# Finishing rows of an expert mixture: one VectorE step in place of two GpSimd steps, GpSimd's work in program order, four buffers for the running sums

## The chip, the core and the metric

The kernel runs on one core of one Trainium2 chip. Its time is the device time of one execution in microseconds. The core has five engines with queues of their own: TensorE (PE, with its weight loads PEld), VectorE (DVE), ScalarE (ACT), GpSimd (POOL) and SyncE (SP). Each runs its queue in order, and waits at the head of it for semaphores of the others. DMAs are issued from the queues (here SP's and POOL's) and run beside the engines.

## The reference, cut to what matters

One decoder layer over 4096 tokens of width 1024: retention and gated DeltaNet heads, an output projection, and then a mixture of experts. The change touches only the mixture and the final norm:

```python
gate = p_group * p_exp / jnp.sum(p_exp, axis=-1, keepdims=True)      # 2 of 32 experts for each token
hid = jax.nn.silu(lax.ragged_dot(xs, w1, group_sizes)) * lax.ragged_dot(xs, w3, group_sizes)
ys = lax.ragged_dot(hid.astype(xs.dtype), w2, group_sizes) * gate.reshape(-1)[order][:, None]
ffn = jax.ops.segment_sum(ys, tok, num_segments=n)                   # the two experts' rows of a token are added
x = x + gate2[:, None, :] * ffn
return rmsnorm(x, final_norm_w)                                      # x * rsqrt(mean(x*x) + 1e-6) * final_norm_w
```

So a token is finished when its second expert has been added: then its row is scaled by one over its root mean square and multiplied by a weight vector.

## The kernel before

Every product is made in three passes over values split into a high and a low part (`split`, L69 to L72: ACT rounds to the high part, DVE subtracts). The expert stage, `phase_d`, is the last of four, and runs from about 2640 us to the end.

The 32 experts are ranked by how many tokens chose them, and each rank has a fixed capacity of rows, from 832 down to 128. They run in the order largest, smallest, second largest, second smallest, and so on. An expert's rows are cut into tiles of up to 128 rows and these into chunks of up to 384 rows, that is 1 to 3 tiles. In the first part of the stage chunks of 256 rows are mixed with experts of one tile of 128 rows; in the last third chunks of 3 tiles (288 or 320 rows) alternate with chunks of 2 tiles (240 rows).

For each chunk:

- `d_gather`: POOL issues one indirect DMA per tile that gathers the chunk's input rows (`xg`, three buffers), L1340. It is called one chunk ahead.
- `d_turn`: PE transposes the rows (`ptx`, L1356), ACT and DVE split them into `xh` and `xl`.
- `d_hidden`: PE multiplies with w1 and w3 (`ph`, L1385 to L1387, or L1414 to L1416 for a tile of 128 rows); ACT and DVE make the hidden values `hs`, `hh`, `hl`. At two points in it, `job` takes up to two waiting pieces of work each.
- `d_acc`: POOL gathers, per tile, the running sums of the chunk's tokens (`ag`, 128 x 1040, L1433) from `acc_d`. Column 1024 says whether the token has been seen. `ag` has three buffers ("rooms").
- `d_to`: POOL works out from that column two row numbers (`to`, L1446 to L1449): one for `acc_d`, one for the output; one of them is always out of range, and the DMA drops such rows.
- `d_rows`: PE multiplies with w2 (`py`, L1478 to L1480), DVE scales (`yg`, L1485) and adds to `ag` (L1486). Then POOL scatters `ag` back to `acc_d` (`keep`, L1513), and `end` is put on a list for the next chunk.
- `end`, per tile: ACT squares and sums the row (`jkD`, `ssD`, L1521), POOL makes the inverse root in seven small steps (`rsqrt_p`, `rp_t`, `rp_h`, `rp_y`, L1325 to L1330), scales the tile in place (L1530), multiplies it with the weights `fw` (L1531), and scatters it to the output (L1532). The room is free when this scatter has read it. The last chunk does this with one DVE step (L1526).

The weights of the next experts are loaded by SP (`rawD`, 12 pieces of 512 KB per expert, L1301) and split by ACT (`whD`, L71) and DVE (`wlD`, L72).

A compile-time scheduler puts the instructions of each engine in order by its own estimate of when their inputs are ready; nothing in the expert stage of the kernel before ties POOL's order down.

Of the kernel before, what the change touches and what calls it, by code (L numbers as in the profile page):

```python
# [53 lines left out]
class Kern:  # L54
# [1064 lines left out]
    def phase_d(self):  # L1119
        tc, nc, T = self.tc, self.nc, self.T  # L1120
        caps = [min(c, T) for c in self.CAPS]
        with tc.tile_pool(name="D", bufs=2) as p:
# [93 lines left out]
            for e in out:  # L1216
                e()
            self.outs = None
            n = nc.values_load(li[0:1, 2 * P:], min_val=0, max_val=P - 1)
            with tc.For_i(0, n, 1) as i:  # L1220
# [20 lines left out]
                self.d_rows(p, s, w, tb, [], [], [], True)  # L1241

    def overflow(self, p, caps):
# [38 lines left out]
        dg, on, limb = (p.tile([P, P], F32, name=nm, bufs=1) for nm in ("dg", "on", "limb"))  # L1282
# [36 lines left out]
    RAWS = 5  # L1319

    def rsqrt_p(self, p, ss, m):

        v = self.nc.gpsimd
        y, t, h = (p.tile([P, 1], F32, name=nm, bufs=2)[0:m] for nm in ("rp_y", "rp_t", "rp_h"))
        v.tensor_scalar(t, ss, 1.0 / D, EPS, op0=ALU.mult, op1=ALU.add)  # L1325
        v.tensor_scalar(h, t, -0.5, 1.0, op0=ALU.mult, op1=ALU.mult)
        v.tensor_tensor(y, t, self.mhalf[0:m], op=ALU.pow)  # L1327
        for _ in range(2):
            v.tensor_scalar(t, y, y, h, op0=ALU.mult, op1=ALU.mult)  # L1329
            v.tensor_scalar(y, t, 1.5, y, op0=ALU.add, op1=ALU.mult)  # L1330
        return y

    def d_gather(self, p, s, ids):
# [3 lines left out]
        for t, m in s["tiles"]:  # L1337
            x = self.xg[self.n_x % len(self.xg)][:, 0:D]
            self.n_x += 1
            nc.gpsimd.indirect_dma_start(out=x[0:m], out_offset=None, in_=self.h2_d,  # L1340
                                         in_offset=bass.IndirectOffsetOnAxis(ap=ids[0:m, t:t + 1], axis=0),
                                         bounds_check=self.T - 1, oob_is_err=False)
            s["x"].append(x)
# [20 lines left out]
    def d_hidden(self, p, s, w, jobs, ends):  # L1364
# [61 lines left out]
    def d_acc(self, p, s, t, m, ids):  # L1426

        nc, T = self.nc, self.T
        agw = p.tile([P, 1040], F32, name="ag", bufs=3)
        if self.n_ag < 3:  # L1430
            nc.gpsimd.memset(agw, 0.0)
        self.n_ag += 1
        nc.gpsimd.indirect_dma_start(out=agw[0:m], out_offset=None, in_=self.acc_d,  # L1433
                                     in_offset=bass.IndirectOffsetOnAxis(ap=ids[0:m, t:t + 1], axis=0),
                                     bounds_check=T - 1, oob_is_err=False)
        s.setdefault("ag", {})[t] = agw

    def d_to(self, p, s, slots):

        v, T = self.nc.gpsimd, self.T  # L1440
        s["to"] = {}
        for t, m in s["tiles"]:
            agw, tok = s["ag"][t], slots[0:m, t, 0:1]
            c = agw[0:m, D:D + 1]
            to = s["to"][t] = p.tile([P, 2], I32, name="to", bufs=4)
            v.tensor_scalar(to[0:m, 0:1], c, float(T), tok, op0=ALU.mult, op1=ALU.add)  # L1446
            v.tensor_scalar(c, c, -float(T), float(T), op0=ALU.mult, op1=ALU.add)
            v.tensor_scalar(to[0:m, 1:2], c, 1.0, tok, op0=ALU.mult, op1=ALU.add)
            v.memset(c, 1.0)  # L1449

    def d_rows(self, p, s, w, slots, turn, jobs, out, last):
# [14 lines left out]
        for q, (t, m) in enumerate(s["tiles"]):  # L1466
# [118 lines left out]
```

## Time and profile before

| what | us |
|---|---|
| median of 3 runs | 4194.59 (4189.52 to 4203.25) |
| the profiled execution | 4198.52 |
| its span, first to last instruction | 4196.3 |
| PE busy over the span | 3927.8 (94%) |
| DVE / ACT / POOL busy over the span | 2430.0 / 1591.0 / 2112.9 |

The profile is of one execution. A busy share over the whole span is a mean over stages, so the rows below are of the expert stage alone, and of stretches in it. "Idle before" is the time in which an engine stood at the instruction, with what ended it. Times are us from the span's start.

### The profile page before, as it was taken

The numbers are of one execution on the slowest core, as the hardware profiler recorded it, in microseconds if no ns is written. First come the engines' busy times: TensorE is split into PE (matmuls) and PEld (weight loads), VectorE is DVE, ScalarE is ACT, GpSimd is POOL, SyncE is SP. The second block draws the span as 40 slices with busy tenths as digits, with TensorE's granted clock in tenths as the row PEclk, the third lists the DMA queues.
The fourth block names the chain that finished last, engine by engine and source line by source line (L and its number), as shares of the span: only waits on it lengthen the run. The fifth ranks groups of instructions, "written<-read, shape, count | busy, mean of one in ns | idle before, by whom it ended". The sixth has DMA issues, their size and how long they took to land. (4 is left out here: it accounts for less than half of the span.)

```text
span 4196.3 us, 73225 instructions
## 1 busy us (share of the span) xinstructions
PE 3927.8 (94%) x27074; PEld 3527.3 (84%) x27074; DVE 2430.0 (58%) x5857; ACT 1591.0 (38%) x3298; POOL 2112.9 (50%) x2834
## 2 busy tenths in 40 slices
PE   5999999999999999889999999599999999998897
PEld 4888889899999999778888887588888888887786
DVE  6555533677777777632222223566666777666675
ACT  3334433544444444422111112244444444443352
POOL 2333333333344433313333333377777788888886
PEclk9999999999999999999999999799999999999999
DMA  6433322422222222553333332456666775666563
GB/s 191 148 122 116 107 90 71 133 48 65 70 72 57 61 65 71 141 155 121 121 121 121 121 121 76 153 177 207 198 194 201 234 239 191 205 195 199 181 225 120
DMA packets 459759, 577.48 MB, mean 138 GB/s; under 512 B 97296, under 2 KB 361720, under 8 KB 459400
## 3 DMA queue, kind: packets, MB, share of 16 engines
q1 hardware_dynamic: 411112, 464.72, 35.9%
q0 software_dynamic: 45632, 102.64, 7.5%
q10 hardware_dynamic: 2656, 5.42, 0.4%
q8 instruction: 214, 3.51, 0.3%
q14 instruction: 145, 1.19, 0.1%
HBM read 458.94 MB, written 166.78 MB: 149 GB/s over the span
## 5 line engine op out<-in xcount | busy, mean ns | idle before, releaser
L1386 PE MATMUL ph<-xl,whD 128*128 128x240 f32 (+7 forms) x2048 | 594.3, 291 | 28.8 <-DVE xl L72 28.5
L1387 PE MATMUL ph<-xh,wlD 128*128 128x240 f32 (+7 forms) x2048 | 591.1, 290 | 0.0
L1385 PE MATMUL ph<-xh,whD 128*128 128x240 f32 (+7 forms) x2048 | 583.6, 291 | 7.0 <-ACT xh L71 3.8
L72 DVE TENSOR_TENSOR wlD<-rawD,whD 128x1024 fp32r<-128x1024 f32 x384 | 514.3, 1355 | 83.8 <-ACT whD L71 77.0
L71 ACT ACTIVATE whD<-rawD 128x1024 fp32r<-128x1024 f32 x384 | 399.2, 1056 | 234.4 <-DMA rawD<-in_w_dram 73.6
L522 PE MATMUL pjB<-hhB,whi 128*128 128x260 f32 x1536 | 444.1, 292 | 10.2 <-DVE cv L530 5.0
L523 PE MATMUL pjB<-hlB,whi 128*128 128x260 f32 x1536 | 441.9, 289 | 4.5 <-DMA hlB<-hl_d 4.5
L524 PE MATMUL pjB<-hhB,wlo 128*128 128x260 f32 x1536 | 442.1, 289 | 0.0
L1386 PEld LDWEIGHTS ph<-xl,whD 128*128 128x128 f32 x2048 | 394.7, 193 | 34.5 <-DVE xl L72 31.8
L1385 PEld LDWEIGHTS ph<-xh,whD 128*128 128x128 f32 x2048 | 389.6, 192 | 14.0 <-ACT xh L71 6.3
L1387 PEld LDWEIGHTS ph<-xh,wlD 128*128 128x128 f32 x2048 | 394.4, 193 | 1.4
L532 POOL TENSOR_TENSOR cv<-cv,cv 128x256 f32<-128x256 f32 x192 | 141.7, 739 | 402.3 <-DVE Xd L602 141.3
L522 PEld LDWEIGHTS pjB<-hhB,whi 128*128 128x128 f32 x1536 | 290.5, 190 | 13.9 <-ACT beta L403 5.1
L523 PEld LDWEIGHTS pjB<-hlB,whi 128*128 128x128 f32 x1536 | 291.5, 190 | 8.8 <-DMA hlB<-hl_d 6.2
L524 PEld LDWEIGHTS pjB<-hhB,wlo 128*128 128x128 f32 x1536 | 291.6, 190 | 1.6
L1478 PE MATMUL py<-whD,hh 128*128 128x512 f32 (+4 forms) x640 | 260.7, 407 | 23.4 <-DVE hh L69 11.1
L1479 PE MATMUL py<-wlD,hh 128*128 128x512 f32 (+4 forms) x640 | 253.6, 396 | 0.0
L1480 PE MATMUL py<-whD,hl 128*128 128x512 f32 (+4 forms) x640 | 247.2, 400 | 4.9 <-DVE hl L72 4.8
L946 DVE TENSOR_TENSOR xC<-poC,xC 128x512 f32<-128x512 f32 x64 | 44.3, 691 | 329.0 <-PE poC L292 328.4
L530 DVE SCALAR_TENSOR_TENSOR cv<-pjB,cw,cv 128x256 f32<-128x256 f32 x384 | 183.1, 479 | 80.2 <-ACT cv L528 72.9
L290 PE MATMUL pgz<-whi,hhC 128*128 128x512 f32 x512 | 206.7, 404 | 5.4 <-DMA hhC<-hh_d 2.9
L1531 POOL TENSOR_TENSOR ag<-ag,fw 128x1024 f32<-128x1024 f32 (+4 forms) x78 | 209.1, 2681 | 5.0
(457 smaller groups left out, 10604.0 us busy)
## 6 DMA issues: line engine op xcount, KB each, us to landing
rawD<-in_w_dram SPq DMA_DIRECT2D x384, 512.0 KB
wa<-in_w_ada_dram SPq DMA_DIRECT2D x48, 512.0 KB
hhB<-hh_d SPq DMA_DIRECT2D x64, 260.0 KB
hlB<-hl_d SPq DMA_DIRECT2D x64, 260.0 KB
acc_d<-xC SPq DMA_DIRECT2D x32, 520.0 KB
wraw<-in_w_in_dram SPq DMA_DIRECT2D x32, 512.0 KB
hh_d<-hh SPq DMA_DIRECT2D x16, 1024.0 KB
hl_d<-hl SPq DMA_DIRECT2D x16, 1024.0 KB
```

What stands on the lines that cost most here:

```text
L71: nc.scalar.activation(hi, src, AF.Copy)
L72: (e_lo or nc.vector).tensor_tensor(lo, src, hi.bitcast(F32) if hasattr(hi, "bitcast") else hi, op=ALU.subtract)
L522: nc.tensor.matmul(pj, wh, hh[k], start=(k == 0), stop=False)
L523: nc.tensor.matmul(pj, wh, hl[k], start=False, stop=False)
L524: nc.tensor.matmul(pj, wl, hh[k], start=False, stop=(k == KD - 1))
L1385: nc.tensor.matmul(ph[nm], hi, xh[:, k, 0:n], start=(k == 0), stop=False)
L1386: nc.tensor.matmul(ph[nm], hi, xl[:, k, 0:n], start=False, stop=False)
L1387: nc.tensor.matmul(ph[nm], lo, xh[:, k, 0:n], start=False, stop=(k == KD - 1))
L1478: nc.tensor.matmul(py[i], a, hi, start=(k == 0), stop=False)
L1479: nc.tensor.matmul(py[i], a, lo, start=False, stop=False)
L1480: nc.tensor.matmul(py[i], b, hi, start=False, stop=(k == 3))
L1531: nc.gpsimd.tensor_tensor(a, a, self.fw[0:m], op=ALU.mult)
```

## The change

For a finished tile the two wide POOL steps (scale, multiply by `fw`) become one DVE instruction, `(ag * ssD) * fw`, in place in `ag`. `end` is cut in two: `norm` (ACT's square, POOL's seven small steps, which now write into `ssD`) runs at the first `job` point of the next chunk's `d_hidden`, and `end` (the DVE step and the scatter to the output) at the second. `ag` has four rooms, and the gathers of the next chunk's sums for which a room is free are called at the first point, the others and `d_to` at the second. Nearly all POOL instructions of the stage are tied, for the scheduler, behind the POOL instruction that was traced before them (`pin`). At the start of the stage the first chunk's row gather is called ahead of the first weight loads. The squares' scrap tile shares its three buffers with `yg`; `ssD` has four, `to` six; two tiles of `overflow` share those of `hs`.

```diff
@@ phase_d
-            out = []
+            out = [[], []]
             load_slots(0)
             load_slots(1)
+            self.d_gather(p, st[0], ids)
             load(order[0], 8)
-            self.d_gather(p, st[0], ids)
...
-                ends, out = out, []
+                ends, out = out, [[], []]
+
+                acc = [lambda t=t, m=m: self.d_acc(p, s, t, m, ids) for t, m in s["tiles"]]
+                free = self.AGS - len(ends[0])
+                ends[0] += acc[:free]
+                ends[1] += acc[free:] + [lambda: self.d_to(p, s, slots)]
                 self.d_hidden(p, s, ex[r], jobs[:2], ends)
-                for e in ends:
-                    e()
-                for t, m in s["tiles"]:
-                    self.d_acc(p, s, t, m, ids)
-                self.d_to(p, s, slots)
@@ constants and helpers
     RAWS = 5
+    AGS = 4
+
+    def pin(self, ins):
+        return self.tc.keep_in_program_order(ins)
@@ d_hidden, job
-            for _ in range(2):
-                if ends:
-                    ends.pop(0)()
+            if ends:
+                for f in ends.pop(0):
+                    f()
@@ d_acc
-        agw = p.tile([P, 1040], F32, name="ag", bufs=3)
+        agw = p.tile([P, 1040], F32, name="ag", bufs=self.AGS)
@@ d_rows
-            def end(agw=agw, to=to, m=m):
-                a = agw[0:m, 0:D]
-                ss = p.tile([P, 1], F32, name="ssD", bufs=3)[0:m]
-                jk = p.tile([P, D], BF, name="jkD", bufs=1)[0:m]
-                nc.scalar.activation(jk, a, AF.Square, accum_out=ss)
+            ss = p.tile([P, 1], F32, name="ssD", bufs=4)[0:m]
+
+            def norm(agw=agw, ss=ss, m=m):
+
+                jk = p.tile([P, D], BF, name="jkD", tag="yg", bufs=3)[0:m]
+                nc.scalar.activation(jk, agw[0:m, 0:D], AF.Square, accum_out=ss)
...
+                else:
+                    self.rsqrt_p(p, ss, ss, m)
+
+            def end(agw=agw, ss=ss, to=to, m=m):
+                a = agw[0:m, 0:D]
+                ot = a
+                if last:
                     ot = p.tile([P, 1024], F32, name="rawD", bufs=self.RAWS)[0:m]
-                    nc.vector.scalar_tensor_tensor(ot, a, ss, self.fw[0:m], op0=ALU.mult, op1=ALU.mult)
-                    a = ot
-                else:
-                    ss = self.rsqrt_p(p, ss, m)
-                    nc.gpsimd.tensor_scalar(a, a, ss, 1.0, op0=ALU.mult, op1=ALU.mult)
-                    nc.gpsimd.tensor_tensor(a, a, self.fw[0:m], op=ALU.mult)
+                nc.vector.scalar_tensor_tensor(ot, a, ss, self.fw[0:m], op0=ALU.mult, op1=ALU.mult)
...
-                out.append(end)
+                out[0].append(norm)
+                out[1].append(end)
```

What this makes of the engines' order is shown at three places. Lines of the changed kernel are a few higher: the row gather is L1343, the sums' gather L1436, the scatter to the sums L1516, the scatter to the output L1539, DVE's addition L1489, and the new DVE step L1538.

First, POOL at the start of the stage, before:

```order
L1266 IOTA col 128x1
L1433 DMA ag<-acc_d,ids 128x1040 x2
L1446 TENSOR_SCALAR to<-ag,slots 128x1
L1447 TENSOR_SCALAR ag<-ag 128x1
L1448 TENSOR_SCALAR to<-ag,slots 128x1
L1449 MEMSET ag 128x1
L1446 TENSOR_SCALAR to<-ag,slots 128x1
L1447 TENSOR_SCALAR ag<-ag 128x1
L1448 TENSOR_SCALAR to<-ag,slots 128x1
L1449 MEMSET ag 128x1
L1340 DMA xg<-h_d,ids 128x1024 x6
```

and in the changed kernel:

```order
L1264 IOTA col 128x1
L1343 DMA xg<-h_d,ids 128x1024 x2
L1436 DMA ag<-acc_d,ids 128x1040 x2
L1343 DMA xg<-h_d,ids 128x1024
L1449 TENSOR_SCALAR to<-ag,slots 128x1
L1450 TENSOR_SCALAR ag<-ag 128x1
L1343 DMA xg<-h_d,ids 128x1024
```

The first chunk's two row gathers (`xg`) moved from behind eight small steps that need the sums (`ag`) landed to the front, ahead of the sums' gathers.

Second, POOL while a chunk of 288 rows (tiles of 128, 128 and 32) is finished beside the hidden part of the chunk of 240 rows (tiles of 128 and 112) that follows it; before, from the scaling of the second tile on:

```order
L1530 TENSOR_SCALAR ag<-ag,rp_y 128x1024
L1531 TENSOR_TENSOR ag<-ag,fw 128x1024
L1513 DMA acc_d<-ag,to 4096x1040
L1532 DMA out_dram<-ag,to 4096x1024
L1325 TENSOR_SCALAR rp_t<-ssD 32x1
L1433 DMA ag<-acc_d,ids 128x1040
L1326 TENSOR_SCALAR rp_h<-rp_t 32x1
L1327 TENSOR_TENSOR rp_y<-rp_t,mhalf 32x1
L1329 TENSOR_SCALAR rp_t<-rp_y,rp_h 32x1
L1330 TENSOR_SCALAR rp_y<-rp_t,rp_y 32x1
L1329 TENSOR_SCALAR rp_t<-rp_y,rp_h 32x1
L1433 DMA ag<-acc_d,ids 112x1040
```

and in the changed kernel, from the scatter of the third tile's sums on:

```order
L1516 DMA acc_d<-ag,to 4096x1040
L1334 TENSOR_SCALAR ssD<-rp_t,rp_y 128x1
L1329 TENSOR_SCALAR rp_t<-ssD 128x1
L1330 TENSOR_SCALAR rp_h<-rp_t 128x1
L1331 TENSOR_TENSOR rp_y<-rp_t,mhalf 128x1
L1436 DMA ag<-acc_d,ids 128x1040
L1333 TENSOR_SCALAR rp_t<-rp_y,rp_h 128x1
L1334 TENSOR_SCALAR rp_y<-rp_t,rp_y 128x1
L1539 DMA out_dram<-ag,to 4096x1024
L1333 TENSOR_SCALAR rp_t<-rp_y,rp_h 128x1
L1334 TENSOR_SCALAR ssD<-rp_t,rp_y 128x1
L1329 TENSOR_SCALAR rp_t<-ssD 32x1
```

The first gather of the next chunk's sums moved from behind the second tile's output scatter to ahead of the first tile's; the wide steps are gone, and the output scatter of a tile now stands behind the small steps of the tile after it.

Third, DVE at the same place, from the hidden values (`hs`, 240 columns) of the chunk of 240 on, before:

```order
L1391 TENSOR_TENSOR hs<-ph,hs 128x240
L1486 TENSOR_TENSOR ag<-ag,yg 32x512
L72 TENSOR_TENSOR wlD<-rawD,whD 128x1024 x3
L72 TENSOR_TENSOR hl_41151<-hs,hh_41147 128x240
L1391 TENSOR_TENSOR hs<-ph,hs 128x240
L72 TENSOR_TENSOR wlD<-rawD,whD 128x1024 x2
L72 TENSOR_TENSOR hl_41152<-hs,hh_41148 128x240
L72 TENSOR_TENSOR wlD<-rawD,whD 128x1024
L1391 TENSOR_TENSOR hs<-ph,hs 128x240
L72 TENSOR_TENSOR hl_41153<-hs,hh_41149 128x240
L72 TENSOR_TENSOR wlD<-rawD,whD 128x1024 x3
L1391 TENSOR_TENSOR hs<-ph,hs 128x240
```

and in the changed kernel:

```order
L1394 TENSOR_TENSOR hs<-ph,hs 128x240
L1489 TENSOR_TENSOR ag<-ag,yg 32x512
L72 TENSOR_TENSOR wlD<-rawD,whD 128x1024 x2
L72 TENSOR_TENSOR hl_41098<-hs,hh_41094 128x240
L1538 SCALAR_TENSOR_TENSOR ag<-ag,ssD,fw 128x1024
L1394 TENSOR_TENSOR hs<-ph,hs 128x240
L72 TENSOR_TENSOR wlD<-rawD,whD 128x1024 x2
L72 TENSOR_TENSOR hl_41099<-hs,hh_41095 128x240
L1538 SCALAR_TENSOR_TENSOR ag<-ag,ssD,fw 128x1024
L72 TENSOR_TENSOR wlD<-rawD,whD 128x1024 x2
L1394 TENSOR_TENSOR hs<-ph,hs 128x240
L1538 SCALAR_TENSOR_TENSOR ag<-ag,ssD,fw 32x1024
```

The three new steps stand between the hidden values and the splits of the next expert's weights, one behind each of the first three parts of the hidden work.

## Rows read from the trace of the kernel before

**Rows 1.** Busy time by stretch (view by windows), three stretches of the expert stage: start and end in us from the span's start, length, then busy us and count of PE, PEld, DVE, ACT and POOL, the granted TensorE clock as a share of 2.4 GHz (mean over the stretch), DMA share and GB/s.
```profile
2637.00:2680.00 43.00, 4.52 (x20) 3.81 (x21) 27.96 (x97) 14.59 (x16) 12.54 (x20) 0.50 0.79 266
2680.00:3450.00 770.00, 743.36 (x5072) 683.37 (x5071) 502.62 (x644) 327.37 (x492) 565.17 (x659) 0.99 0.62 200
3450.00:4060.00 610.00, 546.64 (x3562) 489.17 (x3562) 402.45 (x489) 256.72 (x377) 499.19 (x556) 0.95 0.62 197
```

**Rows 2.** Waits of PE in the expert stage: who waited, for what, us in total, times, longest.
```profile
PE ptx L1356 <- DMA xg<-h_d,ids: 55.3, 6, 31.1
```

**Rows 3.** Timeline of PE between 3460 and 3950 us, the instructions that ended an idle time of over 1 us: start, duration, engine, line, what it does, and in brackets the idle time before it and what ended it.
```profile
3465.97 0.41 PE L1386 MATMUL ph<-xl,whD 128*128 128x320 f32 x1 [2.55 <-DVE xl L72]
...
3558.52 0.63 PE L1386 MATMUL ph<-xl,whD 128*128 128x320 f32 x1 [6.71 <-DVE xl L72]
...
3652.24 0.63 PE L1386 MATMUL ph<-xl,whD 128*128 128x320 f32 x1 [7.77 <-DVE xl L72]
...
3745.30 0.61 PE L1386 MATMUL ph<-xl,whD 128*128 128x288 f32 x1 [6.89 <-DVE xl L72]
...
3831.47 0.43 PE L1356 MATMUL ptx<-K,xg 32*128 32x32 f32 x4 [3.77 <-DVE xl L72]
...
3849.43 1.09 PE L1356 MATMUL ptx<-K,xg 128*128 128x128 f32 x4 [11.04 <-DMA xg<-h_d,ids]
...
3931.89 0.53 PE L1385 MATMUL ph<-xh,whD 128*128 128x288 f32 x2 [1.76 <-ACT xh L71]
...
3944.97 1.09 PE L1356 MATMUL ptx<-K,xg 128*128 128x128 f32 x4 [11.90 <-DMA xg<-h_d,ids]
```

**Rows 4.** Timeline of POOL between 3805 and 3846 us, where the last rows of a chunk of 288 rows are finished while a chunk of 240 runs, and (last row) the addition of DVE that waits in the same place. Columns as in rows 3.
```profile
3805.64 2.34 POOL L1530 TENSOR_SCALAR ag<-ag,rp_y 128x1024 f32<-128x1024 f32 x1
3808.06 3.25 POOL L1531 TENSOR_TENSOR ag<-ag,fw 128x1024 f32<-128x1024 f32 x1
...
3818.97 1.12 POOL L1530 TENSOR_SCALAR ag<-ag,rp_y 128x1024 f32<-128x1024 f32 x1
3820.17 2.39 POOL L1531 TENSOR_TENSOR ag<-ag,fw 128x1024 f32<-128x1024 f32 x1
...
3825.58 1.05 POOL L1433 DMA_INDIRECT ag<-acc_d,ids  x1 [0.33 <-issue]
...
3829.10 1.11 POOL L1433 DMA_INDIRECT ag<-acc_d,ids  x1 [0.45 <-issue]
...
3831.04 1.12 POOL L1530 TENSOR_SCALAR ag<-ag,rp_y 32x1024 f32<-32x1024 f32 x1
3832.24 2.68 POOL L1531 TENSOR_TENSOR ag<-ag,fw 32x1024 f32<-32x1024 f32 x1
...
3844.99 1.08 POOL L1340 DMA_INDIRECT xg<-h_d,ids  x1 [0.65 <-issue]
...
3830.12 0.69 DVE L1486 TENSOR_TENSOR ag<-ag,yg 128x512 f32<-128x512 f32 x1 [8.07 <-DMA ag<-acc_d,ids]
```

**Rows 5.** Busy time by short stretches behind two of the idle times of rows 3; columns as in rows 1.
```profile
3849.00:3851.00 2.00, 1.57 (x7) 1.60 (x8) 0.00 (x0) 0.00 (x0) 1.62 (x5) 0.50 0.44 143
3851.00:3853.00 2.00, 2.00 (x10) 2.00 (x10) 0.00 (x0) 0.00 (x0) 1.43 (x3) 0.50 0.04 15
...
3945.00:3947.00 2.00, 2.00 (x9) 2.00 (x10) 0.00 (x0) 0.00 (x0) 1.80 (x2) 0.50 0.27 45
```

**Rows 6.** Groups of instructions in the expert stage: line, engine, operation, output and inputs, count, then busy us in total, mean ns of one, and idle time of the engine before them. The last row is from the timeline of DVE: the one step with which the last chunk finishes a tile today.
```profile
L1531 POOL TENSOR_TENSOR ag<-ag,fw 128x1024 f32<-128x1024 f32 (+4 forms) x78 | 209.1, 2681 | 5.0
L1530 POOL TENSOR_SCALAR ag<-ag,rp_y 128x1024 f32<-128x1024 f32 (+4 forms) x78 | 96.9, 1243 | 27.1 <-DMA acc_d<-ag,to 21.0
L72 DVE TENSOR_TENSOR wlD<-rawD,whD 128x1024 fp32r<-128x1024 f32 x384 | 514.3, 1355 | 83.8 <-ACT whD L71 77.0 <-issue 2.1 <-PE pth L1403 0.6
L1486 DVE TENSOR_TENSOR ag<-ag,yg 128x512 f32<-128x512 f32 (+4 forms) x160 | 130.0, 827 | 80.7 <-DMA ag<-acc_d,ids 46.9 <-POOL ag L1530 23.6 <-POOL rp_y L1330 3.2
4175.57 1.29 DVE L1526 SCALAR_TENSOR_TENSOR rawD<-ag,ssD,fw 128x1024 f32<-128x1024 f32 x1
```

**Rows 7.** Timelines of DVE and POOL at two places, each pair at the same moment; columns as in rows 3, "x2" and "x3" are runs of equal instructions with their time from first start to last end.
```profile
3000.38 5.30 DVE L72 TENSOR_TENSOR wlD<-rawD,whD 128x1024 fp32r<-128x1024 f32 x2
3001.35 3.25 POOL L1531 TENSOR_TENSOR ag<-ag,fw 128x1024 f32<-128x1024 f32 x1
3006.53 3.48 DVE L72 TENSOR_TENSOR wlD<-rawD,whD 128x1024 fp32r<-128x1024 f32 x3
...
3522.44 3.48 DVE L72 TENSOR_TENSOR wlD<-rawD,whD 128x1024 fp32r<-128x1024 f32 x3
3523.81 5.07 POOL L1329 TENSOR_SCALAR rp_t<-rp_y,rp_h 128x1 f32<-128x1 f32 x1
```

**Rows 8.** Timelines of POOL and PE at the start of the expert stage; columns as in rows 3.
```profile
2650.55 1.06 POOL L1433 DMA_INDIRECT ag<-acc_d,ids  x1 [5.45 <-issue]
...
2658.92 0.27 POOL L1446 TENSOR_SCALAR to<-ag,slots 128x1 int32<-128x1 f32 x1 [5.98 <-DMA ag<-acc_d,ids]
...
2662.19 1.06 POOL L1340 DMA_INDIRECT xg<-h_d,ids  x1 [0.62 <-issue]
...
2668.78 1.94 PE L1356 MATMUL ptx<-K,xg 128*128 128x128 f32 x8 [31.10 <-DMA xg<-h_d,ids]
...
2679.46 1.01 PE L1385 MATMUL ph<-xh,whD 128*128 128x256 f32 x3
```

More of the change, by code (lines that the diff above doesn't have):

```diff
@@ L1240, in phase_d @@
                 self.d_to(p, s, tb)
[L1241 removed]
+                self.d_rows(p, s, w, tb, [], [], None, True)
     def overflow(self, p, caps):
@@ L1281, in overflow @@
         v.tensor_reduce(tot, over, axis=AX.X, op=ALU.add)
-        dg, on, limb = (p.tile([P, P], F32, name=nm, bufs=1) for nm in ("dg", "on", "limb"))
+        dg, on = (p.tile([P, P], F32, name=nm, tag="hs", bufs=2) for nm in ("dg", "on"))
+        limb = p.tile([P, P], F32, name="limb", bufs=1)
         v.tensor_scalar(dg, self.ident, lst[:, 2:3], None, op0=ALU.mult)
@@ L1319, with rsqrt_p @@
     RAWS = 5
-    def rsqrt_p(self, p, ss, m):
-        v = self.nc.gpsimd
-        y, t, h = (p.tile([P, 1], F32, name=nm, bufs=2)[0:m] for nm in ("rp_y", "rp_t", "rp_h"))
-        v.tensor_scalar(t, ss, 1.0 / D, EPS, op0=ALU.mult, op1=ALU.add)
-        v.tensor_scalar(h, t, -0.5, 1.0, op0=ALU.mult, op1=ALU.mult)
-        v.tensor_tensor(y, t, self.mhalf[0:m], op=ALU.pow)
-        for _ in range(2):
-            v.tensor_scalar(t, y, y, h, op0=ALU.mult, op1=ALU.mult)
-            v.tensor_scalar(y, t, 1.5, y, op0=ALU.add, op1=ALU.mult)
-        return y
+    AGS = 4
+    def pin(self, ins):
+        return self.tc.keep_in_program_order(ins)
+    def rsqrt_p(self, p, out, ss, m):
+        v, pin = self.nc.gpsimd, self.pin
+        y, t, h = (p.tile([P, 1], F32, name=nm, bufs=2)[0:m] for nm in ("rp_y", "rp_t", "rp_h"))
+        pin(v.tensor_scalar(t, ss, 1.0 / D, EPS, op0=ALU.mult, op1=ALU.add))
+        pin(v.tensor_scalar(h, t, -0.5, 1.0, op0=ALU.mult, op1=ALU.mult))
+        pin(v.tensor_tensor(y, t, self.mhalf[0:m], op=ALU.pow))
+        for i in range(2):
+            pin(v.tensor_scalar(t, y, y, h, op0=ALU.mult, op1=ALU.mult))
+            pin(v.tensor_scalar(out if i else y, t, 1.5, y, op0=ALU.add, op1=ALU.mult))
     def d_gather(self, p, s, ids):
@@ L1339, in d_gather @@
             self.n_x += 1
-            nc.gpsimd.indirect_dma_start(out=x[0:m], out_offset=None, in_=self.h2_d,
-                                         in_offset=bass.IndirectOffsetOnAxis(ap=ids[0:m, t:t + 1], axis=0),
-                                         bounds_check=self.T - 1, oob_is_err=False)
+            self.pin(nc.gpsimd.indirect_dma_start(out=x[0:m], out_offset=None, in_=self.h2_d,
+                                                  in_offset=bass.IndirectOffsetOnAxis(ap=ids[0:m, t:t + 1], axis=0),
+                                                  bounds_check=self.T - 1, oob_is_err=False))
             s["x"].append(x)
@@ L1444, in d_to @@
             c = agw[0:m, D:D + 1]
[L1445 to L1449, printed above, removed]
+            to = s["to"][t] = p.tile([P, 2], I32, name="to", bufs=6)
+            pin(v.tensor_scalar(to[0:m, 0:1], c, float(T), tok, op0=ALU.mult, op1=ALU.add))
+            pin(v.tensor_scalar(c, c, -float(T), float(T), op0=ALU.mult, op1=ALU.add))
+            pin(v.tensor_scalar(to[0:m, 1:2], c, 1.0, tok, op0=ALU.mult, op1=ALU.add))
+            pin(v.memset(c, 1.0))
     def d_rows(self, p, s, w, slots, turn, jobs, out, last):
@@ L1540, in d_rows @@
             if last:
+                norm()
                 end()
```

23 lines of the change are left out of this document (11 added, 12 removed).

## The prediction, made before the changed kernel was run

> **What bounds the kernel now.** I read the busy time by stretch first, then the waits of PE, then the timelines at the longest of them.
>
> Until the expert stage nothing is touched: it ends at about 2637 us. In the stage PE is the bound most of the time, and what matters is where it is not [rows 1]. There are three such places: the start, where PE is busy for 4.5 of 43 us; the middle (2680 to 3450), with 770 - 743.4 = 26.6 us idle; and the late part (3450 to 4060), with 610 - 546.6 = 63.4 us idle, at a mean clock of 0.95 where the middle has 0.99. What lies behind 4060 I leave as it is.
>
> The waits name one cause for two of the places: PE waited 55.3 us in all for gathered rows (`xg`), 31.1 of it at once [rows 2], and that one is the start [rows 8]. The late part shows eight idle times of over 1 us [rows 3]: 2.6 + 6.7 + 7.8 + 6.9 + 3.8 + 11.0 + 1.8 + 11.9 = 52.4 us. Two end with `xg`, five with `xl`, one with `xh`.
>
> Why these come late is read from POOL. In rows 4 the gathers of the next chunk's sums go out at 3825.58 and 3829.10, and the row gather for which PE then waits at 3844.99. In front of them in POOL's queue stand, for three tiles, a scaling and a multiplication each, of which those shown take 2.34 + 3.25 + 1.12 + 2.39 + 1.12 + 2.68 = 12.9 us. DVE stood 8.07 us at the addition to the sums, and the `xl` that PE needs stands behind that addition. So the late bound is POOL's queue, by two ways: a late row gather, and a late gather of sums that stops DVE.
>
> After a long idle time PE also runs slowly: in the 4 us behind the 11.0 us and the 2 us behind the 11.9 us the granted clock is 0.50, that is 1.2 GHz [rows 5].
>
> **The change, part by part.**
>
> *The wide steps.* POOL loses 78 multiplications at 2.681 us and 78 scalings at 1.243 us, 209.1 + 96.9 = 306 us, 3.9 us per tile [rows 6]. DVE gains 78 steps. The last chunk has that step already, at 1.29 us [rows 6]: 78 x 1.29 = 101 us.
>
> DVE also gets something back. Two weight splits took 5.30 us while POOL multiplied from 3001.35 to 3004.60; three took 3.48 us where POOL did not, 1.16 each [rows 7]. So one such meeting cost DVE 5.30 - 2.32 = 3.0 us, about the whole multiplication. Over the stage a split took 1.355 us on average and an addition 0.827 [rows 6], against 1.16 [rows 7] and 0.69 [rows 4] undisturbed: at most 384 x 0.195 + 160 x 0.137 = 75 + 22 = 97 us. DVE thus ends between 101 us fuller (nothing comes back) and about even. I take even: the meeting in rows 7 is as long as POOL's step itself.
>
> *Late part.* Without 12.9 us of wide steps the row gather at 3844.99 goes out at about 3832, and PE, which waited 11.0 us for it, would not wait. The gathers of sums gain more, since with four rooms the first of them needs no finished tile; in the order of the changed kernel it stands ahead of the first output scatter. DVE's 8.07 us then shrink to what the second gather is late, some 0 to 3 us. I take 85% of the 52.4 us, 44.5 us; bounds: all of it, and half (26 us, first rival). What is late next is the second sums' gather, which still waits for a tile of the chunk before to be scattered.
>
> *Clock.* Five of the idle times are over 6 us. At 0.50 a microsecond loses half of itself: 4 us behind each is 2 us, 5 x 2 = 10 us in all. At 85%, 8.5 us; bounds 0 and 10.
>
> *Start.* In the kernel before the sums' gathers go first, at 2650.55, and have landed when the small steps start at 2658.92; the row gathers go at 2662.19, PE starts at 2668.78, and the first hidden product at 2679.46 [rows 8]. With the row gathers first and the same 8.4 us to land, PE starts at about 2658.9, 9.9 us earlier. If the 10.7 us from there to the first product stay, the gain is 9.9. Part of them is a queue behind weight splits, which is shorter earlier; but the two groups of transposes need 2 x 1.94 us in any case, so at most 9.9 + 10.7 - 3.9 = 16.7. If the first weights are delayed as much as the rows are advanced, nothing is gained. I take 12, nearer to the 9.9 that the rows give. The sums' gathers, moved behind, are needed only after the hidden part.
>
> *Middle.* PE's idle time there stands at the experts of one tile, where DVE is full: two tiles are finished beside each of seven such experts. If both POOL steps meet DVE there, DVE loses 2 x 3.0 before and 2 x 1.29 after: 3.4 us gained, 24 over seven. If none does, 2.6 us are lost each, 18 over seven. I take a gain of 4 us, just above even, since where DVE is full POOL's step can hardly miss it.
>
> *Program order, `job` points, buffers.* Small POOL steps keep their number. The tie adds a wait: a tile's output scatter now stands in POOL's queue until DVE has made the new step, and the sums' gathers and the next row gathers are behind it. DVE's step in turn waits at the head of its queue for POOL's small steps, with the hidden values and weight splits behind it. I price both at nothing in the forecast, because the hidden part's products of the same chunk run on PE beside them; the price without that cover is in the rivals. The shared scrap buffers and the start-up tiles of `overflow` cost nothing I can see: their users are a chunk apart.
>
> *Sum.* 44.5 + 8.5 + 12 + 4 = 69 us. The profiled execution took 4198.5 us, so it would take 4129.5; the median of the runs shown is 3.9 us lower, so the forecast for the median is 4126.
>
> **The rivals.**
>
> *POOL stays slow (first rival).* DVE's weight splits hold POOL as well: one small step, on a tile one element wide, took 5.07 us while three splits ran [rows 7]. The new step reads two tiles too. If each holds POOL for its 1.29 us, a third of the 306 us comes back (101 us), and with the waits on each other half of the late idle time stays. Gain: 12 + 26 + 0, the clock as before: 38 us, 4157. Against it: the row gather in rows 4 has 12.9 us to gain and needs 11. The Trainium skill, "GPSIMD Engine Reference", section 8, says that POOL shares its path to SBUF with VectorE and contends with VectorE instructions that have two SBUF inputs. By that rule the new step is itself such an instruction. The trace agrees for the weight splits, in both directions: 5.30 us on DVE, 5.07 us on POOL.
>
> *DVE waits where it is full (slower).* At the seven experts of one tile two new steps stand among the splits. If POOL's small steps are starved there as in rows 7, once in each of the two refinements, a step arrives 2 x 5.07 = 10.1 us late and DVE stands still, with `hl` and `xl` for PE behind it. That is 14 x 10.1 = 142 us, and 4126 + 142 = 4268. It eats the gain from 69 / 14 = 4.9 us per step on. Against it: as soon as DVE stands, POOL is free again, so one such wait should be over after a few steps.
>
> *The chain only moves (no change).* If POOL, tied in program order, waits at each output scatter for DVE as long as it multiplied before, the late gathers are as late as now and the start alone remains: 4194.6 - 12 = 4183. For it speaks that the wait at the scatter is new; against it, that 1.29 us replace 3.9 us.
>
> **How the numbers follow.** Forecast 0.68, own range 4105 to 4145. First rival 0.16, at 4157. The chain only moves 0.09, at 4183. Slower 0.07, at 4268. The low end takes all bounds together, 52.4 + 10 + 16.7 + 24 = 103 us, 4092. The high end goes to 4168, beyond the first rival; about 0.19 is left out. Differences under 0.3% (12.6 us) can't be told from none here. Faster by more than that: the forecast, nearly all of the first rival and a little of the third, 0.85; within it, most of the third, 0.08; slower 0.07.
>
> **What would show it.** In the profile after: no POOL group of the two wide steps; a DVE group of 78 at 1.29 us; weight splits at about 1.2 us on average in place of 1.355; the first hidden product at about 2667; the late idle times of PE gone but for a few of 1 to 3 us, and a clock near 0.99 there. POOL's idle time before the output scatter is the new wait: over 100 us with PE idle behind it would mean the third rival. DVE idle before the new step, ended by POOL, of over 4.9 us at the experts of one tile would mean the slower one. The forecast is wrong if PE's idle time between 3450 and 4060 stays above 30 us.

## The result and the profile after

The changed kernel took 4256.78 us (median of 4, 4252.25 to 4262.24) against 4194.74 us before, 1.0146 times as long (95% interval 1.0126 to 1.0167): 62 us slower, where 4126 us, 69 us faster, had been forecast. The profiled execution has a span of 4260.4 us, 64.1 us more than before.

Busy time by stretch of the changed kernel, the stretches and columns of [rows 1]:

```profile
2637.00:2680.00 43.00, 14.08 (x84) 12.90 (x85) 27.08 (x111) 13.50 (x17) 19.08 (x23) 0.57 0.68 234
2680.00:3450.00 770.00, 707.33 (x4722) 650.18 (x4721) 464.30 (x648) 307.21 (x462) 397.67 (x562) 0.95 0.59 191
3450.00:4060.00 610.00, 558.70 (x3530) 491.57 (x3529) 378.24 (x503) 246.27 (x373) 381.94 (x470) 0.94 0.58 189
2600.00:4275.00 1675.00, 1468.58 (x9571) 1318.56 (x9569) 1016.54 (x1592) 645.95 (x976) 919.59 (x1216) 0.93 0.57 184
```

and the whole stage of the kernel before, for the last of these rows:

```profile
2600.00:4275.00 1675.00, 1429.27 (x9563) 1294.34 (x9561) 1037.92 (x1514) 655.17 (x976) 1188.73 (x1370) 0.95 0.57 184
```

The start gains: TensorE is busy for 14.1 of the 43 us, 4.5 before. But the middle, which had been full, loses 36 us of TensorE's busy time, and the late stretch is busier by 12 us without getting further: fewer products run in it than before (3530 records, 3562 before). Over the whole stage TensorE is busy 39.3 us longer for the same products (1468.58 against 1429.27 us), with a mean clock of 0.93 against 0.95; the rest of the 64 us is idle time. By the clock records of the two traces TensorE was busy at the low level, 0.50, for 55.5 us of the stage before and for 135.6 us now. Half of the 80.1 us between them is 40 us, so the clock alone makes the 39.3 us; in the late stretch it is half of 59.2 - 31.2, 14 us. All other engines are busy for less time than before.

The waits of VectorE and of TensorE in the stage (waits view: total us, times, longest):

```profile
DVE ag L1538 <- POOL ssD L1334: 249.7, 75, 9.3
DVE yg L1488 <- PE py L1483: 159.3, 79, 5.1
DVE hs L1394 <- PE ph L1390: 74.6, 27, 4.4
...
PE py L1483 <- DVE hl L72: 45.8, 18, 5.3
PE ptx L1359 <- DVE xl L72: 31.8, 15, 5.8
PE ptx L1359 <- DMA xg<-h_d,ids: 21.0, 1, 21.0
PE ph L1388 <- DVE hs L1394: 19.7, 8, 4.4
```

The first line is new and the longest of VectorE in total: it stands 249.7 us, at 75 of the 78 new steps, for the last of GpSimd's small steps. The line for `xg` says that the late waits for gathered rows of [rows 2, 3] are gone, but for the one at the start. In their place TensorE waits for `hl` (4.8 us before) and `hs` (2.5 us before), which VectorE makes; its waits for `xl`, VectorE's too, are about as long as before (31.8 and 5.1 us, 13.8 and 28.5 before). The groups of [rows 6], as they are now:

```profile
L1538 DVE SCALAR_TENSOR_TENSOR ag<-ag,ssD,fw 128x1024 f32<-128x1024 f32 (+4 forms) x78 | 100.2, 1284 | 249.7 <-POOL ssD L1334 249.7
L72 DVE TENSOR_TENSOR wlD<-rawD,whD 128x1024 fp32r<-128x1024 f32 x384 | 460.5, 1220 | 46.3 <-ACT whD L71 37.8 <-PE py L1483 4.8 <-ACT xh L71 2.1
L1489 DVE TENSOR_TENSOR ag<-ag,yg 128x512 f32<-128x512 f32 (+4 forms) x160 | 107.8, 686 | 1.9
L1329 POOL TENSOR_SCALAR rp_t<-ssD 128x1 f32<-128x1 f32 (+4 forms) x78 | 101.8, 1305 | 92.0 <-ACT jkD L1526 87.1
```

One expert of one tile shows how it goes, GpSimd's timeline first, then VectorE's and TensorE's (start, us; in brackets the idle time before and what ended it), then two short stretches with TensorE's busy time as the first column and the granted clock as the third from the end:

```profile
3098.54 3.12 POOL L1330 TENSOR_SCALAR rp_h<-rp_t 128x1 f32<-128x1 f32 x1
...
3103.90 1.03 POOL L1516 DMA_INDIRECT acc_d<-ag,to  x1 [0.44 <-issue]
3104.96 0.28 POOL L1334 TENSOR_SCALAR ssD<-rp_t,rp_y 128x1 f32<-128x1 f32 x1
3105.32 1.28 POOL L1329 TENSOR_SCALAR rp_t<-ssD 96x1 f32<-96x1 f32 x1
...
3113.13 0.27 POOL L1334 TENSOR_SCALAR ssD<-rp_t,rp_y 96x1 f32<-96x1 f32 x1
```

```profile
3099.26 2.34 DVE L72 TENSOR_TENSOR wlD<-rawD,whD 128x1024 fp32r<-128x1024 f32 x2
3105.28 1.28 DVE L1538 SCALAR_TENSOR_TENSOR ag<-ag,ssD,fw 128x1024 f32<-128x1024 f32 x1 [3.67 <-POOL ssD L1334]
3106.48 2.35 DVE L72 TENSOR_TENSOR wlD<-rawD,whD 128x1024 fp32r<-128x1024 f32 x2
3108.75 0.42 DVE L1425 TENSOR_TENSOR hs<-ph,hs 128x256 f32<-128x256 f32 x1
3109.08 0.28 DVE L72 TENSOR_TENSOR hl<-pth,hh 128x128 fp32r<-128x128 f32 x1
...
3113.43 1.28 DVE L1538 SCALAR_TENSOR_TENSOR ag<-ag,ssD,fw 96x1024 f32<-96x1024 f32 x1 [2.93 <-POOL ssD L1334]
3114.63 1.27 DVE L72 TENSOR_TENSOR xl<-ptx,xh 128x512 fp32r<-128x512 f32 x2
```

```profile
3109.42 1.22 PE L1483 MATMUL py<-whD,hl 128*128 128x512 f32 x2 [4.01 <-DVE hl L72]
...
3115.37 0.90 PE L1359 MATMUL ptx<-K,xg 128*128 128x128 f32 x3 [3.02 <-DVE xl L72]
```

```profile
3108.00:3110.00 2.00, 0.58 (x1) 0.50 (x2) 2.00 (x4) 0.60 (x2) 1.89 (x2) 0.50 0.64 145
...
3122.00:3124.00 2.00, 2.00 (x11) 2.00 (x11) 0.85 (x4) 0.00 (x0) 1.47 (x3) 0.50 1.02 360
```

A small step on a tile one element wide took 3.12 us while VectorE ran two weight splits and the steps around them, a scatter of the sums stands between the small steps, and the scale is there at 3105.24. VectorE goes on at 3105.28; the `hl` that TensorE needs stands behind the step and two splits. The second tile's chain takes 8.1 us (3105.32 to 3113.40), VectorE stands again, and now `xl` is late. The first step of that chain took 1.28 us, as long as the new VectorE step beside it. TensorE loses 4.01 + 3.02 us, and its granted clock is 0.50, the 1.2 GHz level, from 3108 to 3124.

### The profile page after: what moved, and what is told of

Same layout as the page of the kernel before. It is cut to its first block, busy times and chain, and to the rows that moved or that the text cites. A ratio compares the mean times of both kernels' runs of the same rounds, so it can differ in the third digit from the quotient of the medians.

```text
span 4260.4 us, 73114 instructions
## 1 busy us (share of the span) xinstructions
PE 3966.5 (93%) x27074; PEld 3550.6 (83%) x27074; DVE 2410.4 (57%) x5935; ACT 1582.8 (37%) x3298; POOL 1844.4 (43%) x2679
## 4 chain that ended last, share of the span: by engine, by line
PE 70%; POOL 8%; DVE 8%; DMA 7%; issue 4%; ACT 2%; SPq 1%; POOLq 0%; DVEq 0%; ACTq 0%
PE ph L1389 4%; PE ph L1388 4%; PE ph L1390 4%; PE pjB L523 3%; PE pjB L522 3%; PE pjB L524 3%; PE py L1481 3%; PE py L1482 3%; PE pgz L291 3%; PE pgz L292 3%; PE pgz L290 3%; PE poC L291 3%; PE poC L290 3%; PE poC L292 3%; PE py L1483 3%
## 5 line engine op out<-in xcount | busy, mean ns | idle before, releaser
L1388 PE MATMUL ph<-xh,whD 128*128 128x240 f32 (+7 forms) x2048 | 588.0, 293 | 21.1 <-DVE hs L1394 19.7
L72 DVE TENSOR_TENSOR wlD<-rawD,whD 128x1024 fp32r<-128x1024 f32 x384 | 460.5, 1220 | 46.3 <-ACT whD L71 37.8
L1388 PEld LDWEIGHTS ph<-xh,whD 128*128 128x128 f32 x2048 | 393.2, 194 | 29.3 <-DVE hs L1394 21.6
L522 PEld LDWEIGHTS pjB<-hhB,whi 128*128 128x128 f32 x1536 | 290.5, 190 | 14.7 <-DMA hhB<-hh_d 5.1
L1483 PE MATMUL py<-whD,hl 128*128 128x512 f32 (+4 forms) x640 | 256.0, 415 | 45.9 <-DVE hl L72 45.8
L1538 DVE SCALAR_TENSOR_TENSOR ag<-ag,ssD,fw 128x1024 f32<-128x1024 f32 (+4 forms) x78 | 100.2, 1284 | 249.7 <-POOL ssD L1334 249.7
L290 PE MATMUL pj<-whi,hh 128*128 128x512 f32 x512 | 206.0, 402 | 6.2 <-ACT whi L71 6.1
```

What stands on the lines that cost most here:

```text
L72: (e_lo or nc.vector).tensor_tensor(lo, src, hi.bitcast(F32) if hasattr(hi, "bitcast") else hi, op=ALU.subtract)
L290: nc.tensor.matmul(out, a, hi, start=(k == 0), stop=False)
L522: nc.tensor.matmul(pj, wh, hh[k], start=(k == 0), stop=False)
L1388: nc.tensor.matmul(ph[nm], hi, xh[:, k, 0:n], start=(k == 0), stop=False)
L1483: nc.tensor.matmul(py[i], b, hi, start=False, stop=(k == 3))
```

## The experiments

All times are medians; ratios are to the kernel before, timed on the same chip, with their 95% interval. Line numbers shift by a few with the edits. Theory A: VectorE's wait is the price. Rival B: VectorE's added work is. Rival C: GpSimd's fixed order, the two parts and the rooms are.

**The wait, the work, the order.** Four kernels from the changed one, the third from the one before:

```diff
e1  -  scalar_tensor_tensor(ot, a, ss, self.fw[0:m], ...)
    +  scalar_tensor_tensor(ot, a, ss if last else self.mhalf[0:m], self.fw[0:m], ...)
e2  -  nc.vector.scalar_tensor_tensor(ot, a, ss, self.fw[0:m], ...)
    +  self.pin(nc.gpsimd.tensor_scalar(a, a, ss, 1.0, ...))              # where not last
    +  self.pin(nc.gpsimd.tensor_tensor(a, a, self.fw[0:m], ...))
e3  -  nc.gpsimd.tensor_scalar(a, a, ss, 1.0, ...); nc.gpsimd.tensor_tensor(a, a, self.fw[0:m], ...)
    +  nc.vector.scalar_tensor_tensor(a, a, ss, self.fw[0:m], ...)
e4  -  return self.tc.keep_in_program_order(ins)
    +  return ins
```

> The changed kernel, but VectorE's new step multiplies by a constant (-0.5) in place of the row's scale from GpSimd, in all chunks but the last: the small steps still run, the scaling by them is left out, and VectorE no longer waits for GpSimd there. Theory A (VectorE stands 249.7 us at this step for GpSimd's last small step, and the hidden products behind it come late): the wait is gone, granted clock in the middle back near 0.98, 4115 to 4170 us. Rival B (the 100 us of added VectorE work itself is the price): 4230 to 4260 us, VectorE idle less but TensorE as late as before. Rival C (GpSimd in program order, the two parts and the four rooms are the price): 4225 to 4260 us.

> The changed kernel, but the scale and the weighting are done by GpSimd again in two wide steps (2.7 and 1.2 us), at the place where VectorE's step stood and in program order. Theory A: VectorE does not wait for GpSimd any more, 4165 to 4215 us, with the late waits for the gathered rows back. Rival B: the same as A here (the VectorE work is gone too). Rival C (order, parts and rooms are the price): 4235 us or more.

> The kernel before, with only the two wide GpSimd steps replaced by the one VectorE step: old order on GpSimd, one part, three rooms. Theory A: VectorE waits for the last small step here as well, over 150 us in all, 4210 to 4275 us. Rival B: also 4210 to 4275 us, but VectorE's idle time before the step is small. Rival C: the step alone gains, 4110 to 4185 us.

> The changed kernel without the program order on GpSimd (the scheduler places its steps freely); two parts and four rooms stay. Theory A: the small steps still end after VectorE has come to its step, wait 150 to 300 us, 4215 to 4265 us. Rival C (the fixed order makes the small steps late): wait under 100 us, 4120 to 4195 us. Rival B: 4225 to 4265 us whatever the wait.

e1: 4235.36 us, 1.0078 (1.0050 to 1.0106). e2: 4186.93, 0.9968 (0.9953 to 0.9982). e3: 4213.77, 1.0029 (1.0015 to 1.0043). e4: 4250.78, 1.0112 (1.0083 to 1.0142).

With the wide steps on GpSimd, the fixed order, the parts and the rooms together are no loss (e2, 0.9968, which is what the start alone gives, below), and without the fixed order the loss stays (e4). So the loss needs the VectorE step. One thing in e2 was not as I expected: the late waits for gathered rows did not come back (20.5 us for `xg`, all at the start); TensorE waited for `xl` in place of them:

```profile
PE ph L1389 <- DVE xl L72: 41.1, 14, 9.5
```

The step alone, in the kernel before (e3), costs 0.3%, about 12 us. Its time is near the low end of what theory A gave, and it stands for the same two things, 185 us in all:

```profile
DVE ag L1530 <- POOL rp_y L1330: 134.1, 54, 6.6
DVE ag L1530 <- DMA acc_d<-ag,to: 50.9, 16, 7.6
```

So e3 is 43 us faster than the changed kernel, though it has not the gain at the start. The fourth room is not the reason (e12, below) and the fixed order is not (e4: 215.8 us of waits for the scale). What is left is the cut of `end` in two, with the places where its parts are called, and the smaller edits; these were not tried alone.

e1 went against theory A: without the wait for the scale most of the loss was still there, and the clock in the middle came to 0.96 only. Its waits and one step (timeline of VectorE) say why:

```profile
DVE ag L1538 <- DMA acc_d<-ag,to: 168.2, 42, 9.3
```

```profile
3802.03 1.29 DVE L1538 SCALAR_TENSOR_TENSOR ag<-ag,mhalf,fw 128x1024 f32<-128x1024 f32 x1 [7.47 <-DMA acc_d<-ag,to]
```

The step writes in place, into the room that the scatter of the sums still reads, so it can have to wait for that as well. e1 met this wait because the scheduler, with no scale to wait for, placed the step earlier: between a tile's last addition and its step VectorE runs 6 instructions (median of the 78 steps), 9 in the changed kernel, and it comes to the step 3.6 us after the scatter was issued, 9.2 us in the changed kernel. Theory A became A2: VectorE stands for whichever of the two comes last, because the step is placed ahead of both.

**Both waits, and each.** Leaving VectorE's result unread needs a tile more, and room for it: three rooms in all three kernels.

```diff
e12 -  AGS = 4
    +  AGS = 3
e13 as e12, and where not last:
    +  junk = p.tile([P, 1024], F32, name="otD", bufs=1)[0:m]
    +  scalar_tensor_tensor(junk, a, self.mhalf[0:m], self.fw[0:m], ...)
e15 as e13, with ss for self.mhalf[0:m]
```

> The changed kernel with three rooms for sums in place of four, nothing else. The three-room kernel with the old order and the VectorE step took 4213.77 us. If the fourth room is what costs the 43 us between that and the changed kernel: 4205 to 4225 us. If it is the two parts and the program order: 4245 to 4275 us, with additions waiting for their gather.

> The changed kernel with three rooms, and VectorE's step (same size and place in the program) multiplies by a constant and writes into a tile that nobody reads, so that it waits for nobody; the rows go out unscaled. VectorE's work is all there. Theory A2: 4120 to 4175 us, VectorE idle before the step under 20 us. Rival B2: 4215 to 4260 us.

> The changed kernel with three rooms; VectorE's step multiplies by GpSimd's scale again, but writes into a tile that nobody reads, and the rows go out unscaled. So of the two waits that for the small steps is there, and that for the scatter's landing is gone. If each wait alone costs nearly what both do (they end at about the same time): 4205 to 4245 us, with 150 to 240 us of idle time before the step. If the scatter is what counts: 4140 to 4175 us. If the two add up: 4175 to 4205 us.

e12: 4245.63 us, 1.0099 (1.0082 to 1.0117). e13: 4141.62, 0.9858 (0.9841 to 0.9874). e15: 4249.80, 1.0108 (1.0079 to 1.0137), with this wait:

```profile
DVE otD L1542 <- POOL ssD L1334: 227.6, 73, 7.7
```

This settles it between the theories. e13 has all of VectorE's work (1016.92 us in the stage, 1016.54 in the changed kernel) and no wait, and is 60 us faster than before; rival B falls (e14b, below, has the work, with the right result, and is faster still). In the text e15 differs from it by the scalar operand alone, and takes 108 us more. But the operand also moves the step: in e13 one VectorE instruction stands between a tile's last addition and its step (median), in e15 ten. One tile of e13 (timeline of VectorE):

```profile
3104.10 0.68 DVE L1489 TENSOR_TENSOR ag<-ag,yg 128x512 f32<-128x512 f32 x1
3104.70 0.42 DVE L72 TENSOR_TENSOR hl<-hs,hh 128x256 fp32r<-128x256 f32 x1
3105.03 1.28 DVE L1542 SCALAR_TENSOR_TENSOR otD<-ag,mhalf,fw 128x1024 f32<-128x1024 f32 x1
```

So the 108 us are the price of the wait together with the place at which the scheduler lets the step wait; these runs don't part the two.

The wait for the scale by itself costs what both cost (e12). The reason that I gave for this case, that the two waits end at about the same time, does not hold in the changed kernel: its trace has the landing of the scatter for 45 of the tiles, and at every one of them the scatter had landed before the scale was there, by 0.4 to 20.4 us, 8.4 in the median. There the scale was the only wait; the scatter became one where the step moved ahead (e1). Three rooms are no slower than four here; by the two ratios to before rather half a per cent faster. e12's time is in the range for the two parts and the program order, so the fourth room is not the price; but no addition waited for its gather there, as that range had it.

**The small steps.** e6 leaves five of GpSimd's seven small steps out of the changed kernel:

```diff
-  h = t * -0.5;  y = pow(t, -0.5);  twice: t = y * y * h;  y = (t + 1.5) * y
+  out = pow(t, -0.5)
```

> The changed kernel with two of GpSimd's seven small steps for a tile's scale, the first and the power: the step that halves the mean and the two rounds of refinement (four steps) are left out. If the length of the chain is what makes the scale late: wait for it under 120 us; but the scatter's landing stands behind it (168.2 us when the scale was a constant), so 4225 to 4250 us all the same. If the chain's length sets the price: 4150 to 4200 us.

4165.18 us, 0.9906 (0.9889 to 0.9922), with these waits:

```profile
DVE ag L1537 <- POOL ssD L1330: 41.6, 33, 2.8
DVE ag L1537 <- DMA acc_d<-ag,to: 36.2, 18, 4.3
```

The scatter did not step into the gap as I had expected from e1: the length of the chain is most of the price. Five small steps fewer per tile take 249.7 - 41.6 - 36.2 = 172 us of waits from VectorE and 92 us from the kernel (4256.78 - 4165.18). A reservation: GpSimd is also busy for 182 us less (738.04 against 919.59 us in the stage), and this run doesn't part that from the wait.

**The place of the step.** In the text the step stands behind the hidden part, but nothing held it there on VectorE. e8 holds it, e10 adds the square and the small steps straight behind the additions, e14a and e14b move the step at experts of one tile (there `s["rows"]` is empty; `old` is the number of finished tiles that wait), e17 is e14b without e10's edit, e16 has e14b's move without the hold, e10's edit and the new order in `job`.

```diff
e8   -  nc.vector.scalar_tensor_tensor(ot, a, ss, ...)
     +  self.pin(nc.vector.scalar_tensor_tensor(ot, a, ss, ...))
     (and in job() the ends run ahead of the load)
e10  -  out[0].append(norm)
     +  norm()
e14  +  s["fin"] = [];  if not s["rows"]: s["fin"], ends[1] = ends[1][:old], ends[1][old:]
     +  for f in s.pop("fin", []): f()    # e14a: behind s["late"](), the late splits; e14b: behind both add(i), the additions
```

> The changed kernel with VectorE's new step held in program order too: it stands behind the last hidden split of the next chunk, not among the hidden products' steps where the scheduler had put it (the step's job runs ahead of the weight load's job for that). Theory A2 (VectorE stands at the step for two things one behind the other, GpSimd's last small step and the landing of the scatter that still reads the same room, because the step is placed ahead of both, and hidden products wait behind it): idle time before the step under 100 us, 4120 to 4185 us. Rival B2 (added VectorE work and its effect on GpSimd's small steps): 4215 to 4260 us. Rival D (the step later makes rooms late, so that additions wait for their gather): step's idle gone, but additions wait over 80 us for a gather, 4190 to 4260 us.

> As the run before (the step behind the last hidden split), and ScalarE's square and GpSimd's small steps straight behind the additions of the same tile, not in the next chunk. Theory A2: 4115 to 4180 us, no more than 10 us from the run before, since the step has all inputs by then. Rival D: 4190 to 4260 us.

> The 4186.1 us kernel (VectorE's step in program order behind the last hidden split, square and small steps straight behind the additions), and at one-tile experts the step one place later: behind the two hidden splits that come late there, ahead of the evictions. Theory A2 (what is left of the loss sits at the one-tile experts, where the step still stands in front of late splits): TensorE's middle stretch from 701 to over 725 of 770 us busy, 4140 to 4175 us. Rival D (the step now delays evictions and rooms instead): 4180 to 4215 us.

> As the run before, but at one-tile experts the step stands behind the additions. Theory A2: 4135 to 4175 us, as the run before or better, since neither splits nor evictions are behind the step. Rival D: the next chunk's first split comes late in their place, 4180 to 4215 us.

> The changed kernel with VectorE's step (and the scatter behind it) behind the additions at one-tile experts, in the program's text alone: nothing holds the step in program order on VectorE, so the scheduler may place it ahead again, as it does elsewhere. If the place in the text is enough at one-tile experts and most of the loss sits there: 4140 to 4190 us. If it is the scheduler's placing of the step among the hidden steps, there and at wider chunks: 4225 to 4260 us, wait for the small steps still over 150 us.

> The 4115.15 us kernel with the square and the small steps in the next chunk's first hidden job, as in the changed kernel; the step stays behind the last hidden split and, at one-tile experts, behind the additions. If the place of the step is all: 4110 to 4125 us. If the early square counts as it did without the move at one-tile experts (4207.66 against 4186.1 us): 4130 to 4145 us, with 20 to 60 us of waits for the small steps.

e8: 4207.66 us, 1.0017 (1.0007 to 1.0028). e10: 4186.10, 0.9968 (0.9956 to 0.9979). e14a: 4129.59, 0.9825 (0.9796 to 0.9854). e14b: 4115.15, 0.9789 (0.9759 to 0.9818). e16: 4260.65, 1.0142 (1.0125 to 1.0159). e17: 4138.25, 0.9852 (0.9835 to 0.9868).

Held behind the hidden splits, the step waits 58.2 us for the scale in e8 and 26.4 in e10, yet both stayed above what I expected of A2 (and e10 was 22 us faster than e8, not within 10), and rival D's late additions (26.4 and 32.2 us of waits for a gather) did not explain it. e10's other wait is 18.0 us for the scatter. All eleven of its waits, 44 us, lie between 2812 and 3420 us, around the experts of one tile, and TensorE's longest idle times after the start stand right behind them; one of them (VectorE's step, then TensorE's product):

```profile
3119.60 1.29 DVE L1538 SCALAR_TENSOR_TENSOR ag<-ag,ssD,fw 128x1024 f32<-128x1024 f32 x1 [6.64 <-DMA acc_d<-ag,to]
...
3122.28 1.22 PE L1483 MATMUL py<-whD,hl 128*128 128x512 f32 x2 [7.52 <-DVE hl L72]
```

By e10's stretches (the first two rows below) the late part was mended and the middle was not; by e14b's (the last two) both are:

```profile
2680.00:3450.00 770.00, 701.48 (x4658) 642.66 (x4657) 458.88 (x640) 303.33 (x455) 383.87 (x549) 0.94 0.59 189
3450.00:4060.00 610.00, 594.96 (x3976) 533.46 (x3975) 433.51 (x575) 285.66 (x420) 424.01 (x532) 1.00 0.67 217
```

```profile
2680.00:3450.00 770.00, 748.44 (x5090) 686.40 (x5089) 507.15 (x707) 333.06 (x500) 429.93 (x601) 0.99 0.63 206
3450.00:4060.00 610.00, 595.35 (x4036) 535.37 (x4035) 438.81 (x579) 291.41 (x428) 436.55 (x545) 0.99 0.68 220
```

The middle is where the experts of one tile are, and moving the step there alone brought 71 us (4186.10 to 4115.15), more than I expected of it; e14a too is faster than its range (737.13 us busy in the middle, over 725 as expected). In e14b the step waits 0.7 us in all. e16 shows that the move in the text is nothing without the hold: the wait was 240.9 us again. The early square (e17 to e14b) brings 23 us, though the wait for the scale was already down to 14.7 us in e17. The middle is the same in both (749.07 and 748.44 us busy); the difference is in the late part, where e17 has TensorE waiting up to 4.8 us for `yg`, which stands on VectorE behind such a step:

```profile
3520.31 1.27 DVE L1544 SCALAR_TENSOR_TENSOR ag<-ag,ssD,fw 64x1024 f32<-64x1024 f32 x1 [2.48 <-POOL ssD L1338]
3521.52 0.73 DVE L1492 SCALAR_TENSOR_TENSOR yg<-py,slots,g 128x512 f32<-128x512 f32 x1
...
3522.31 0.77 PE L1485 MATMUL py<-whD,hh 128*112 128x512 f32 x1 [4.59 <-DVE yg L1492]
```

These waits for `yg` are 21.1 us in e17 and 10.5 in e14b, so they are a part of the 23 us; the rest is open.

**The start alone**, in the kernel before:

```diff
-  load(order[0], 8)
   self.d_gather(p, st[0], ids)
+  load(order[0], 8)
```

> The kernel before with the first chunk's gather ahead of the first expert's load, nothing else. The prediction's term for the start was a gain of 9.9 to 16.7 us, 12 taken: 4182 to 4191 us against 4194 to 4201 for the kernel before. If the start's gain is taken back later: within 3 us of the kernel before.

4186.26 us, 0.9965 (0.9951 to 0.9979), against 4202.48: a gain of 16 us, the interval 9 to 21. In its profiled execution the first hidden product starts at 2674.19, 5.3 us earlier than in the kernel before, so the trace doesn't show the whole of the gain.

## Why the prediction was wrong

The step that failed is the one on program order, `job` points and buffers: "DVE's step in turn waits at the head of its queue for POOL's small steps, with the hidden values and weight splits behind it. I price both at nothing in the forecast, because the hidden part's products of the same chunk run on PE beside them". The cover does not hold: each hidden product goes through VectorE (`hs`, then `hl`) before TensorE can go on, and these are the very steps that stand behind the wait. In the expert shown above VectorE stood until 3105.28, and TensorE had run out of products and was idle until 3109.42. Over the stage VectorE stood 249.7 us. The price was about 108 us (e15 less e13, the wait with the place it gives the step), and with the step held behind the work that TensorE needs it was gone (e14b).

The other steps against the runs:

- *Wide steps.* Right. A new step took 1284 ns (1.29 forecast), a split 1220 ns ("about 1.2"), an addition 686 ns. VectorE was taken as even and came out 21 us emptier (1016.54 against 1037.92 us). One reading was loose: the small step of 5.07 us in [rows 7] ran to 3528.88, beyond the three splits named, beside two more (3526.48 to 3528.82).
- *Late part and clock.* Reached in e14b: TensorE's busy time from 3450 to 4060 rises by 595.35 - 546.64 = 48.7 us (44.5 forecast), at a clock of 0.99. That the wait goes is not enough: in e13 it rises by 21.6 us (568.25), at 0.96, with two late waits for gathered rows left (9.5 and 10.3 us). Nor are the wide steps the whole cause of the late row gathers: with them on GpSimd, e2 has no late wait for `xg` either. In the changed kernel the idle time there was 51 us, over the 30 set as the sign of a wrong forecast.
- *Clock, the other way.* Not priced: many idle times of 1 to 6 us held the clock at its low level for stretches that had been at full speed, 0.95 in the middle where [rows 1] has 0.99.
- *Start.* Right in its mechanism; TensorE starts at 2660.68 (2658.9 forecast) and with the first hidden product at 2670.13 ("about 2667"), by the timeline of the changed kernel, so 9.3 us of the 12 show there. 16 us alone by the medians, with 12 inside the interval.
- *Middle.* 748.44 against 743.36 us in e14b: a gain of 5 us, 4 taken.
- *Sum.* 69 us forecast; 60 without the waits (e13) and 87 with the step in a later place (e14b). That these lie around 69 does not make the terms right one by one.

Of the rivals, the slower one came true, at 4268 forecast and 4256.78 measured, with a chance of 0.07. Its mechanism, VectorE standing for small steps with `hl` and `xl` behind it, is what the trace shows; its place and its size are not. It spoke of 14 steps at 10.1 us; there were 75 at 249.7 / 75 = 3.3 us. At the seven experts of one tile there were 16 (beside two of them three tiles are finished); they wait 1.4 to 3.7 us each, 46 us together, so the sign set for it (over 4.9 us there) did not show. The longest wait, 9.3 us, is in the late part. The argument against it, that GpSimd is free again as soon as VectorE stands, is true (a small step takes 0.2 to 0.6 us then) but there are seven in a row, and scatters with waits of their own among them. That its time came near is luck: too few steps and too long a wait nearly cancelled.

The first rival's mechanism shows too. Of the 78 first small steps, 40 ran beside a new VectorE step and took 1.28 us in the median, 0.18 us being the least; another small step took 3.12 us beside the two splits. This agrees with the rule of the Trainium skill, "GPSIMD Engine Reference", section 8, that the prediction names. But GpSimd kept most of its gain: 1188.73 - 919.59 = 269 of the 306 us, so 37 us came back and not 101. The third rival's wait at the output scatter is 19.2 us for the new step, where over 100 was its sign.

## What to carry to other kernels

When work moves from an engine off the critical path to one in the middle of it, price its waits there, not only its duration: in an engine that works in order, everything behind a waiting step waits too, and a cover counts only if it does not pass through that engine. A step with several inputs from elsewhere is worth moving to behind the work that others wait for, and it must be held there if a scheduler places it; here that turned a loss of 62 us into a gain of 87. When removing a wait gains little, look in the new trace at where the scheduler has put the step, and what it waits for there, before giving up the theory.

## What the runs showed of the chip that I had not expected

- Short idle times cost twice. In the changed kernel no wait of TensorE in the stage but that at the start is over 5.8 us, and the granted clock still fell to 0.50 for stretches such as 3108 to 3124; its busy time in the stage rose by 39.3 us.
- Five steps of one element per row, hardly any arithmetic, decided 92 us (e6). Their time depends on the neighbour: the first of the seven took 180 ns at the least and 1305 ns on average, and 40 of the 78 ran beside the new VectorE step, mostly for as long as it did, 1.28 us.
